# A hybrid recurrent layer: the framework orders the instructions by its other timing model

## The chip, the cores and the metric

The kernel runs on one core of one Trainium2 chip. The metric is the device time of one execution in microseconds (us). Three executions of the kernel before took 660.12, 658.99 and 655.33 us; the median is 658.99.

The core has five engines that run side by side, each from an instruction queue of its own that is worked off strictly in order: TensorE (PE: matmuls; PEld: the loading of a matmul's stationary operand), VectorE (DVE), ScalarE (ACT), GpSimd (POOL) and SyncE (SP), which here only starts transfers (DMA). An instruction that needs another engine's result waits for a semaphore, and all that stands behind it in the same queue waits with it.

## The reference

One layer mixes 1,024 prompt tokens and eight samples of eight tokens each (1,088 tokens of width 1,024). A projection with `w_in` gives the inputs of four mixers and their gates. Mixer A is a causal convolution and a gated linear recurrence (RG-LRU). B is a convolution and a state space model in chunks (SSD). C is a convolution and a gated delta rule in chunks, with one triangular matrix to invert for each chunk and head. D is a complex linear recurrence (S5) with a GELU and a gate. The four gated outputs are put side by side, projected with `w_out`, added to the scaled input and normalised:

```python
z = jnp.einsum('bld,de->ble', x, p['w_in'])
...
ya, conv_a, h_a = rglru_mixer(a_x, conv_a, h_a, p)
yb, conv_b, h_b = ssd_mixer(b_xbc, b_dt, conv_b, h_b, p)
yc, conv_c, s_c = gdn_mixer(c_qkv, c_beta, c_decay, conv_c, s_c, p)
yd, s5_re, s5_im = s5_mixer(d_u, s5_re, s5_im, p)
...
mix = jnp.concatenate([ya, yb, yc, yd], axis=-1).astype(x.dtype)
out = jnp.einsum('ble,ed->bld', mix, p['w_out'])
x = layer_norm(ALPHA * x + out, p['ln_g'], p['ln_b'])
```

Besides the layer's output the new convolution caches and recurrent states are returned. All of it is float32.

## The kernel before

**The large products.** Every float32 operand of a large product is split into two parts, high and low (`xh`, `xl`, `wh`, `wl`), and a product takes three matmuls: lines 261 to 263 for the projection in (tiles `pg`, columns in blocks of 320, 384 and 384, eight k-tiles), lines 438 to 440 for the token-major columns, lines 1511 to 1513 for the projection out. The weights come by DMA into `wr` (two buffers) and are split by ACT (line 157) and DVE (line 158). Two banks of PSUM take the results (`pg`), and ACT or DVE copies them out (lines 277, 279, 1417, 1418).

**The stages.** First come the loads of x, its transposes (line 216) and D's u; then D itself (`s5`), in turn with the token-major columns and the first channel tiles of C; then the decays (`decays`, `softplus`: small DVE steps in a row, lines 337 to 351), and the rest of C's input with its convolutions (lines 299 and 301). From then on two streams are written in turn by `merge`: `gdn` (C's chunks) and `side` (A, then B, the gates, and at the end `project`, the projection out with residual and LayerNorm).

**The chain of C.** For each of nine chunks `invert` doubles an inverse in up to six levels. One level is a chain across engines: PE line 920 (`T`), DVE line 922, two DVE copies line 911 (`tb`), PE lines 925 and 927 (`XY`), ACT line 929, PE line 932, ACT line 933, two DVE copies line 911 (`yb`). Then PE lines 939 to 951 (`E`, `F`) and 961, 964. `state` carries the state from chunk to chunk; `finish` normalises a chunk's output `o`: its factor `ors` is a power taken on POOL (line 1064), DVE applies it (lines 1065, 1068), and PE transposes the result (line 1071, `oT`). `ssd` does the same with `yrs` on POOL (line 1195), DVE line 1196 and the transpose `yT` (line 1200). The LayerNorm of `project` takes its power on POOL too (line 1522), and POOL multiplies and adds two rows of 1,024 (lines 1528 and 1529). A's recurrence needs POOL's line 1295, then a DVE scan (line 1296), then POOL's copies into `hfin` (lines 1297, 1298), which PE transposes (line 1303, `hf`). POOL also copies the convolutions' tails (lines 305, 306), which PE transposes (line 326, `pt`).

**What sets the order.** No order is written out for an engine. The kernel is traced once, and an instruction's place in what was traced is its priority: earlier is more urgent. When the context on line 1569 closes, the framework's planner plays the program on a timing model of the core. Whenever an engine is free in that model, it takes the most urgent of its instructions whose inputs and buffers the model says are ready; an instruction that is less urgent but ready goes ahead of one that still waits. The order in which the model dispatches them is then fixed as the order of each engine's queue on the chip, DMA starts included, and buffers of the rotating pools (for instance the 11 strips of pool `dp`, the two `wr`, the two banks `pg`) are given out in that same order. Data dependencies hold in any order, by semaphores. In the program before, 2,776 of TensorE's 3,806 instructions and 1,380 of DVE's 1,399 stand at another place in their queue than the written order would give them, by 23 and 30 places on average.

The framework has two such models. The default one, used before, is the simpler. The other is called by the framework "the more detailed of its two timing simulators". Of their differences it says that the default one leaves out the fixed cost of GpSimd's elementwise instructions, and that the other takes every table of ScalarE's functions as loaded, so that it sees no cost in a change of tables; the default one does price that.

Of the kernel before, what the change touches and what calls it, by code (L numbers as in the profile page):

```python
# [22 lines left out]
T = NP + NS  # L23
# [10 lines left out]
def seqs(ap):  # L34
    """[p, 88] -> [p, seq, 11]: three cached columns, then eight tokens."""
    return ap.rearrange("p (b e) -> p b e", e=11)
# [7 lines left out]
def hybrid_step(ctx, tc, I, O, dbg=None):  # L44
    nc = tc.nc
# [6 lines left out]
    I = {k: v[0] if k not in ("x_prompt", "x_sample") else v for k, v in I.items()}  # L52
# [51 lines left out]
    def merge(*streams):  # L104
        """Emits several streams in step, each by its share of its own length: (generator, length)."""
        live = [[g, 0.0, w] for g, w in streams]
        while live:
            e = min(live, key=lambda e: e[1] / e[2])
            try:
                c = next(e[0])  # L110
                e[1] += c
                yield c
            except StopIteration:
                live.remove(e)
# [10 lines left out]

# [1 line left out]
    xs2 = I["x_sample"].rearrange("b j d -> (b j) d")  # L127
# [7 lines left out]
    w_in = I["w_in"].rearrange("(k p) e -> p k e", p=P)  # L135
# [3 lines left out]
    def load_w(parts, kn=4, pool=None):  # L139
        """Columns of w_in in two exact parts: the views of each k-tile."""  # L140
        n = sum(b - a for a, b in parts)
# [20 lines left out]

# [1 line left out]
    eps6 = 1e-6  # L164
# [7 lines left out]

# [1 line left out]
    prm = strip(cc, name="prm")  # L174
# [28 lines left out]

# [1 line left out]
    xh = xp.tile([P, 8, T], F32R, name="xh", tag="xh")  # L205
# [13 lines left out]

# [1 line left out]
    pcol = const([P, off[6]], F32, "pcol")  # L221
# [15 lines left out]
    def col(key, i):  # L237
        """Column i of a parameter: channel tile (and tap, for the convs)."""
        j, t = divmod(i, tiles_of.get(key, 6))
        c = off[t] + rows[key] + j  # L240
        return pcol[:, c:c + 1]
# [4 lines left out]

# [1 line left out]
    deep = [0, 0]  # L248
# [32 lines left out]
    def gemm_strip(c0, key, i, pool):  # L281
        """A projected channel tile laid out for the causal conv."""
        s = strip(pool, name="z")
        G.memset(s[:, 0:3], 0.0)
        G.tensor_copy(seqs(s[:, 1027:SW])[:, :, 0:3], cached(key, i))

        def evac(a, b, o):
            if a == 0:
                copy_out(seqs(s[:, 1027:SW])[:, :, 3:11], toks(o[:, :NS]))
                copy_out(s[:, 3:3 + b - NS], o[:, NS:])  # L290
            else:
                copy_out(s[:, 3 + a - NS:3 + b - NS], o)

        yield from gemm_ch(c0 + P * i, evac)
        return s
# [12 lines left out]
    def silu_compact(s, acc):  # L308
        """acc holds half the conv: silu = (tanh(acc) + 1) acc, samples first."""
        a0, s0 = seqs(acc[:, NP:CL])[:, :, 3:11], toks(s[:, 0:NS])  # L310
        act(s0, a0, AF.Tanh)
        act(s[:, NS:T], acc[:, :NP], AF.Tanh)
        stt(s0, s0, 1.0, a0, OP.add, OP.mult)
        stt(s[:, NS:T], s[:, NS:T], 1.0, acc[:, :NP], OP.add, OP.mult)
# [4 lines left out]
    def store_tails(gt, nt, oi):  # L319
        """[p, nt, 27] -> conv caches: three rows of the prompt, 24 of the samples."""  # L320
        t = 0
# [11 lines left out]
    def softplus(x, n):  # L333
        """max(x, 0) + log1p(exp(-|x|)), the log as 2 atanh(u / (2 + u))."""
        nx = small([P, n], name="nx")
# [18 lines left out]
    def exp_fine(o, x, n):  # L354
        """exp to float32's own accuracy: 2^k times a series in the remainder."""
        magic = 1.5 * 2.0 ** 23
# [18 lines left out]
    def rsqrt_fine(o, x, n):  # L375
        """1 / sqrt(x) for positive x: a guess from the exponent, then Newton's steps."""
        b = small([P, n], name="b")
# [10 lines left out]

# [1 line left out]
    ud_d = [dr.tile([P, 8, 136], F32, name=f"dud{i}", tag=f"dud{i}") for i in range(2)]  # L390
# [14 lines left out]
    def u_tiles():  # L405
        """u, its tokens in the order (place in the chunk of 8, chunk), through DRAM to [(s, j), g, c]."""
        us = [strip(dp, name="us")[:, :T].rearrange("p (s c) -> p s c", s=8) for _ in range(2)]
# [18 lines left out]

# [1 line left out]
    raw = const([P, 9, 12], F32, "raw")  # L428
# [21 lines left out]
    def decays(x, bias, na):  # L450
        """softplus(x + bias), its running sum times -a within a chunk, and that sum's exponentials."""
        xb = small([P, 9, 4], name="xb")
# [29 lines left out]

    # ================= D: S5 =================
    magic = 1.5 * 2.0 ** 23
# [3 lines left out]
    def s5(dp):  # L488
# [6 lines left out]
        def cmul(o, a, b, sh, e0=V, e1=V, conj=False):  # L495
            """o = a * b or conj(a) * b, each a pair (re, im)."""
            n = math.prod(sh)
# [57 lines left out]
        act(un[:, 1], rr, AF.Sin)  # L555
        # powers of A = mag * unit: A^0 .. A^8
        pw = early([P, 2, 9, 8], F32, "pw")
# [7 lines left out]

        # f = (A - 1) / lambda and B-bar = f * b
        am = small([P, 8], name="am")
# [21 lines left out]
        for r_ in range(2):  # L589
            for s in range(8):  # L590
                G.tensor_copy(pwr[:, r_, :, s], pw[:, r_, 7 - s])
            V.tensor_copy(pwa[:, r_].rearrange("p q s -> p s q"), pw[:, r_, 1:9])
        # the unit's eighth power, brought back to modulus one
        u2 = small([P, 2, 8], name="u2")
# [10 lines left out]
        for j in range(2):  # L605
            tt(u8[:, j], u8[:, j], nr, OP.mult)
        # C transposed: [(g2, n), ri, q, i], with the imaginary part negated too
        ck = dk("ck")
# [5 lines left out]
        ts(ctr[:, 2], pc[:, P:256], -1.0, None, op0=OP.mult)  # L614
        # D on the diagonal of the zero lag: rows (7, j)
        drow = s5in[:, 514:770]
# [5 lines left out]
        dv = dm.rearrange("p (q g i) -> p q g i", q=8, g=2)  # L622
        # initial states of the samples
        hin = early([P, 2, 64], F32, "hin")
# [12 lines left out]
        def sums(hf):  # L637
            """The stationary operands of the sums into a chunk's end state, and the lags' kernels."""
            q0 = 4 * hf
# [41 lines left out]
        def table(hf):  # L681
            """The unit's powers 8, 16, .. 1024, by doubling."""
            q0 = 4 * hf
# [10 lines left out]
        def half_run(hf, U, lg, lo, tz, tab):  # L694
# [18 lines left out]
            cmul((H[:, 0, :, 9:], H[:, 1, :, 9:]), tab, (gd[:, 0], gd[:, 1]), [4, P], V, V)  # L713
            # states after the last token
            for r_ in range(2):
# [47 lines left out]
        yield  # L763
        # GLU: twice the gated output
        glu = strip(dp, name="glu")[:, :512].rearrange("p (k f) -> p k f", k=2)
# [23 lines left out]

# [1 line left out]
    def gammas(wk, ti, ac, nac, heads, ptag, stag, bufs):  # L791
        """exp(ac_t - ac_s) for t >= s in the same run, else 0: [s, head, t]."""
        n = NS if ti == 0 else P
# [13 lines left out]

    # ================= C: gated DeltaNet =================
    HO = (0, 2, 1, 3)   # order of the heads in a tile of four: by half of the partitions

    def norms(tiles, pool):
        """1 / norm of each head's vector, token-major: [t, chunk, head]."""
        ps = bank("ssq")
# [13 lines left out]
    def gdn(wk, up, q, k, v, rk, rq):  # L827
# [65 lines left out]
        def invert(d):  # L893
            """((I + N)^-1)^T from (I + N)^T: blocks of 64 by doubling in half precision and one correction
            from the exact residual, then the two halves joined."""
            n, A = d["n"], d["A"]
# [207 lines left out]

    # ================= B: SSD =================
    def ssd(wk, up, x, BT, CT):
# [152 lines left out]

    # ================= A: RG-LRU =================  # L1260
    def rglru(wk, up, xc, out):
# [46 lines left out]

# [1 line left out]
    U_ = []  # L1310
# [5 lines left out]

# [1 line left out]
    tri = early([P, P], F32, "tri")  # L1318
# [93 lines left out]
    def gate(c0, pool):  # L1412
        """Twice the silu of a gate's tile."""
        g = strip(pool, name="gate")

        def evac(a, b, o):
            act(g[:, a:b], o, AF.Tanh, scale=0.5)
            stt(g[:, a:b], g[:, a:b], 1.0, o, OP.add, OP.mult)

        yield from gemm_ch(c0, evac)  # L1420
        return g
# [43 lines left out]

# [1 line left out]
    def project():  # L1467
# [105 lines left out]
```

## Time and profile before

| | |
|---|---|
| three executions | 660.12, 658.99, 655.33 us |
| median | 658.99 us |
| profiled execution: span, first to last instruction (the page gives no other time for it) | 655.5 us |
| mean granted TensorE clock, share of full | 0.977 |
| busy: PE, PEld, DVE, ACT, POOL | 610.6, 521.9, 483.0, 274.0, 183.9 us |
| instructions | 12,071 |
| HBM read, written | 32.31, 10.41 MB |

"Busy" is the union of the time in which an engine has an instruction under way; TensorE's matmuls overlap in their pipeline, so a busy TensorE need not be at its peak. A wait of an engine is put down to the instruction that released it. Waits of an engine that is not the bound of a stretch cost nothing by themselves.

### The profile page before, as it was taken

Reading aid. Unit: us, or ns where it says so; the run is one execution under the profiler, and the core shown is the slowest. Engines: PE = TensorE matmul, PEld = TensorE weight load, DVE = VectorE, ACT = ScalarE, POOL = GpSimd, SP = SyncE. Lnnn points to the kernel's source line nnn. Section 1 sums busy time; section 2 is a strip of 40 time slices with the busy share of each in tenths; the row PEclk is TensorE's granted clock in tenths of the full one; section 3 lists DMA queues with packets and bytes.
Section 4 is the critical chain, followed back from the end, with each engine's and each line's share of the span. In section 5 each row is a group of like instructions: output and inputs, shape, how many; then the busy total and the mean of one; then the engine's idle time right before and its main releaser. Section 6 shows DMA issues by size and latency. Waiting matters only on the chain.

```text
span 655.5 us, 12071 instructions
## 1 busy us (share of the span) xinstructions
PE 610.6 (93%) x4394; PEld 521.9 (80%) x4394; DVE 483.0 (74%) x1399; ACT 274.0 (42%) x693; POOL 183.9 (28%) x320
## 2 busy tenths in 40 slices
PE   5999899899999999988999999999999796999995
PEld 5999899899998876777888877778878554678884
DVE  5587999955568677798887687868777887854343
ACT  4343335254434254855444434454443742332210
POOL 7511439300202021232302123023030212443533
PEclk9999989899889999998999999999999997999998
DMA  8655003042411111101111132001022511013122
GB/s 248 164 143 159 17 26 101 0 116 60 111 43 37 34 35 33 33 3 31 34 33 33 37 99 72 17 18 42 9 73 73 170 45 48 13 58 123 70 108 84
DMA packets 52569, 43.49 MB, mean 66 GB/s; under 512 B 17051, under 2 KB 45746, under 8 KB 52510
## 3 DMA queue, kind: packets, MB, share of 16 engines
q1 hardware_dynamic: 51966, 42.53, 22.2%
q8 instruction: 34, 0.56, 0.3%
q0 software_dynamic: 544, 0.19, 0.2%
q14 instruction: 25, 0.20, 0.1%
HBM read 32.31 MB, written 10.41 MB: 65 GB/s over the span
## 4 chain that ended last, share of the span: by engine, by line
PE 69%; DVE 20%; issue 4%; ACT 3%; POOL 2%; DMA 2%; SPq 0%; DVEq 0%; ACTq 0%; POOLq 0%
PE pg L261 10%; PE pg L262 10%; PE pg L263 10%; PE pg L1513 5%; PE pg L1511 5%; PE pg L1512 5%; DVE acc L301 2%; DVE tb L911 2%; DVE yb L911 2%; PE ssq L820 1%; PE px L216 1%; DMA x<-in_x_prompt_dram 1%; PE kq L882 1%; PE yd L1158 1%; PE cb L1147 1%
## 5 line engine op out<-in xcount | busy, mean ns | idle before, releaser
L261 PE MATMUL pg<-xh,wh 128*128 128x384 f32 (+1 forms) x480 | 166.9, 348 | 2.2 <-DVE z L279 2.2
L262 PE MATMUL pg<-xl,wh 128*128 128x384 f32 (+1 forms) x480 | 165.8, 345 | 0.0
L263 PE MATMUL pg<-xh,wl 128*128 128x384 f32 (+1 forms) x480 | 164.5, 343 | 0.0
L261 PEld LDWEIGHTS pg<-xh,wh 128*128 128x128 f32 x480 | 92.8, 193 | 5.1 <-DVE z L279 2.8
L262 PEld LDWEIGHTS pg<-xl,wh 128*128 128x128 f32 x480 | 92.7, 193 | 2.7 <-issue 1.3
L263 PEld LDWEIGHTS pg<-xh,wl 128*128 128x128 f32 x480 | 92.6, 193 | 1.2 <-issue 0.3
L1511 PE MATMUL pg<-woh,wh 128*128 128x512 f32 (+1 forms) x144 | 59.0, 409 | 2.5 <-ACT wh L1500 2.5
L1513 PE MATMUL pg<-woh,wl 128*128 128x512 f32 (+1 forms) x144 | 58.8, 408 | 0.4 <-DVE wl L1501 0.4
L1512 PE MATMUL pg<-wol,wh 128*128 128x512 f32 (+1 forms) x144 | 58.9, 409 | 0.0
L301 DVE SCALAR_TENSOR_TENSOR acc<-z,pcol,acc 128x1112 f32<-128x1112 f32 x36 | 49.7, 1380 | 2.7 <-ACT acc L299 2.5
L157 ACT ACTIVATE wh<-wr 128x512 fp32r<-128x512 f32 (+1 forms) x44 | 27.7, 631 | 48.7 <-PE pg L262 33.2
L158 DVE TENSOR_TENSOR wl<-wr,wh 128x512 fp32r<-128x512 f32 (+1 forms) x44 | 31.5, 717 | 13.4 <-ACT wh L157 12.8
L929 ACT ACTIVATE XY<-XY 128x256 f16<-128x256 f32 (+1 forms) x51 | 19.4, 380 | 51.5 <-PE XY L927 46.1
L1514 DVE SCALAR_TENSOR_TENSOR y<-y,pg 128x512 f32<-128x512 f32 (+1 forms) x18 | 12.3, 686 | 32.7 <-PE pg L1513 29.7
L1511 PEld LDWEIGHTS pg<-woh,wh 128*128 128x128 f32 (+1 forms) x144 | 26.9, 187 | 9.7 <-ACT wh L1500 2.8
L1513 PEld LDWEIGHTS pg<-woh,wl 128*128 128x128 f32 (+1 forms) x144 | 26.8, 186 | 7.6 <-DVE wl L1501 0.9
L1512 PEld LDWEIGHTS pg<-wol,wh 128*128 128x128 f32 (+1 forms) x144 | 26.8, 186 | 6.5 <-issue 0.6
L922 DVE TENSOR_TENSOR T<-T,lev 128x256 f16<-128x256 f32 (+1 forms) x51 | 21.4, 420 | 11.3 <-PE T L920 10.6
L277 ACT ACTIVATE z<-pg 128x384 f32<-128x384 f32 (+2 forms) x37 | 14.2, 393 | 35.3 <-PE pg L263 33.9
L933 ACT ACTIVATE XY<-XY 128x256 f16<-128x256 f32 (+1 forms) x51 | 19.5, 381 | 20.5 <-PE XY L932 20.3
L911 DVE COPY tb<-T 64x256 f16<-64x256 f16 x99 | 26.8, 271 | 1.6
L911 DVE COPY yb<-XY 64x256 f16<-64x256 f16 x99 | 23.8, 240 | 5.2 <-ACT XY L933 3.8
(486 smaller groups left out, 1369.6 us busy)
## 6 DMA issues: line engine op xcount, KB each, us to landing
wr<-in_w_in_dram SPq DMA_DIRECT2D x40, 256.0 KB
x<-in_x_prompt_dram SPq DMA_DIRECT2D x8, 512.0 KB
wo<-in_w_out_dram SPq DMA_DIRECT2D x16, 256.0 KB
y<-in_x_prompt_dram SPq DMA_DIRECT2D x8, 512.0 KB
out_dram<-y SPq DMA_DIRECT2D x7, 512.0 KB
bgd<-bg SPq DMA_DIRECT2D x9, 128.0 KB
dud<-us SPq DMA_DIRECT2D x2, 544.0 KB
U<-dud SPq DMA_DIRECT2D x16, 68.0 KB
```

The source lines that it names most:

```text
L157: act(hv_, wv, AF.Copy)
L158: lo_eng[0].tensor_tensor(lv, wv, hv_.bitcast(F32), OP.subtract)
L261: mm(o, whi[k], xh[:, k, a:b], start=(k == 0), stop=False)
L262: mm(o, whi[k], xl[:, k, a:b], start=False, stop=False)
L263: mm(o, wlo[k], xh[:, k, a:b], start=False, stop=(k == 7))
L301: stt(acc[:, :CL], s[:, j:j + CL], col(wkey, j * nt + i), acc[:, :CL], OP.mult, OP.add)
L911: V.tensor_copy(dst[s, :, s], src[s])
L922: tt(t_[:n], pt[:n], lev[:n, l].unsqueeze(1).to_broadcast([n, 4, 64]), OP.mult)
L933: act(XY[:n, 256:], px[:n, 256:], AF.Copy)
L1511: mm(ps[:n], mh[k_], woh[:, k_, e], start=(k_ == 0), stop=False)
L1512: mm(ps[:n], mh[k_], wol[:, k_, e], start=False, stop=False)
L1513: mm(ps[:n], ml[k_], woh[:, k_, e], start=False, stop=(k_ == 7))
```

## The change

The context that closes over the whole kernel is asked to plan on the other timing model. Comments and docstrings are taken out as well (their lines stay empty, so line numbers agree); no other line of code differs.

```diff
@@ -32,7 +32,7 @@
 def seqs(ap):
-    """[p, 88] -> [p, seq, 11]: three cached columns, then eight tokens."""
+
     return ap.rearrange("p (b e) -> p b e", e=11)
...
@@ -1566,7 +1566,7 @@
         outs.append(nc.dram_tensor(f"out_{i}_dram", shape, F32, kind="ExternalOutput").ap())
-    with tile.TileContext(nc) as tc:
+    with tile.TileContext(nc, schedule_with_timeline_sim=True) as tc:
         hybrid_step(tc, ins, outs)
```

So the same instructions with the same operands are issued: none is added and none is removed by the source. What can differ is the order of each of the five queues, which buffer of a pool a tile gets, the semaphores that follow from the two, and how often ScalarE has to load a function table.

## Rows read from the trace of the kernel before

**Rows 1.** the page, busy time of each engine: us, share of the span, instructions.

```profile
PE 610.6 (93%) x4394; PEld 521.9 (80%) x4394; DVE 483.0 (74%) x1399; ACT 274.0 (42%) x693; POOL 183.9 (28%) x320
```

**Rows 2.** stretches: from:to, length, busy us of each engine (instructions), clock, DMA share, GB/s.

```profile
0.00:20.00 20.00, 13.44 (x69) 12.51 (x70) 12.05 (x36) 9.65 (x18) 14.77 (x38) 1.00 0.72 212
...
75.00:125.00 50.00, 44.61 (x305) 42.47 (x304) 48.85 (x128) 15.35 (x40) 32.93 (x64) 0.93 0.16 47
...
275.00:300.00 25.00, 19.56 (x153) 16.92 (x153) 22.53 (x45) 13.36 (x24) 9.06 (x17) 1.00 0.05 11
...
500.00:550.00 50.00, 40.41 (x280) 28.32 (x281) 42.39 (x126) 25.10 (x74) 11.40 (x10) 0.93 0.27 86
...
640.00:655.50 15.50, 7.86 (x34) 6.00 (x32) 5.77 (x10) 0.67 (x1) 5.79 (x3) 0.89 0.18 69
```

**Rows 3.** the page, chain of work that ended last, shares by engine.

```profile
PE 69%; DVE 20%; issue 4%; ACT 3%; POOL 2%; DMA 2%; SPq 0%; DVEq 0%; ACTq 0%; POOLq 0%
```

**Rows 4.** waits of PE: line, releaser, us in total, times, longest us.

```profile
PE XY L927 <- DVE yb L911: 6.0, 4, 5.0
...
PE XY L932 <- DVE tb L911: 2.5, 3, 1.7
...
PE hf L1303 <- POOL hfin L1298: 2.3, 1, 2.3
...
PE F L947 <- DVE tb L942: 1.8, 4, 0.9
...
PE oT L1071 <- DVE o L1068: 1.6, 2, 1.1
...
PE XY L927 <- DVE T L922: 1.6, 2, 1.2
...
PE pt L326 <- POOL tails L305: 1.3, 2, 0.9
...
PE yT L1200 <- DVE y L1196: 0.6, 2, 0.4
```

**Rows 5.** groups of POOL: line, op, shapes, count, busy us, mean ns, idle before.

```profile
L1529 POOL TENSOR_TENSOR y<-y,ln 128x1024 f32<-128x1024 f32 (+1 forms) x8 | 19.4, 2421 | 0.6
...
L1064 POOL TENSOR_TENSOR ors<-oss,mexp 128x4 f32<-128x4 f32 (+1 forms) x9 | 11.2, 1239 | 28.6 <-DVE oss L1062 28.4
```

**Rows 6.** timeline of POOL from 290 us: start us, us, instruction, idle before.

```profile
294.60 2.05 POOL L1064 TENSOR_TENSOR ors<-oss,mexp 128x4 f32<-128x4 f32 x1 [7.40 <-DVE oss L1062]
296.57 0.23 POOL L1295 COPY gi<-pcol 128x8 f32<-128x8 f32 x1
```

**Rows 7.** timeline of PE, three places.

```profile
299.74 0.28 PE L1303 MATMUL hf<-idf,hfin 128*9 128x128 f32 x1 [2.32 <-POOL hfin L1298]
...
547.58 0.40 PE L927 MATMUL XY<-T,yb 128*128 128x64 f16 x4 [5.03 <-DVE yb L911]
547.79 0.78 PE L1513 MATMUL pg<-woh,wl 128*128 128x512 f32 x1
...
580.49 0.41 PE L1071 MATMUL oT<-idf,o 128*128 128x128 f32 x2 [1.12 <-DVE o L1068]
```

**Rows 8.** timeline of DVE from 542 us.

```profile
542.36 2.51 DVE L911 COPY tb<-T 64x256 f16<-64x256 f16 x2
544.90 2.63 DVE L911 COPY yb<-XY 64x256 f16<-64x256 f16 x2
```

**Rows 9.** timeline of POOL from 542 us.

```profile
542.45 2.33 POOL L1528 TENSOR_TENSOR y<-y,ln 64x1024 f32<-64x1024 f32 x1 [1.54 <-ACT y L1527]
544.86 2.33 POOL L1529 TENSOR_TENSOR y<-y,ln 64x1024 f32<-64x1024 f32 x1
```

**Rows 10.** the page, the copies of line 911 on DVE.

```profile
L911 DVE COPY tb<-T 64x256 f16<-64x256 f16 x99 | 26.8, 271 | 1.6
```

**Rows 11.** groups of ACT, two of nine table loads.

```profile
L554 ACT ACT_TABLE_LOAD x1 | 1.3, 1283 | 0.0
L444 ACT ACT_TABLE_LOAD x1 | 1.3, 1283 | 0.0
```

## The prediction, made before the change was run

> **What bounds the kernel now.** I read the busy times first, then the stretches, then the chain of waits, and last the waits of TensorE one by one. TensorE is busy for 610.6 of 655.5 us [rows 1], so it is without any work for 44.9 us. No change of order can return more than that, except for what hides inside busy time (below). Take the idle time apart by stretch, length minus busy [rows 2]: 6.6 us stand in the first 20 us and 7.6 us in the last 15.5 us, where the loads of x and the last tile's LayerNorm leave nothing to put in; 5.4 us stand between 75 and 125 us, where DVE is busy 48.85 of 50 us and is the bound. That leaves 44.9 - 6.6 - 7.6 - 5.4 = 25.3 us, of which 5.4 us between 275 and 300 us and 9.6 us between 500 and 550 us. The chain that ended last agrees: 69% of it is TensorE and 20% DVE [rows 3].
>
> The waits of TensorE say what those 25.3 us are. They are not waits of the large products for weights, in the main, but small matmuls of a chain that stood at the head of the queue before their input was there [rows 4]: the doubling of C's inverse behind DVE's copies (6.0, 2.5, 1.8 and 1.6 us), and transposes that come after a GpSimd step (`hf` 2.3, `oT` 1.6, `pt` 1.3, `yT` 0.6 us). In the order as it runs, matmuls of the projections stand behind them in the same queue: after the longest of these waits, of line 927 until 547.58 us, the third matmul of an open group follows (line 1513), whose first two ran before the wait [rows 7]. So these are errors of the plan: the model thought the input would be there.
>
> One is easy to follow. At 294.60 us GpSimd starts the power `ors`, which takes 2.05 us although it writes 4 elements a partition; the copy for A's recurrence comes only after it [rows 6], DVE's scan waits for the copy, and the transpose `hf` waits 2.32 us at the head of TensorE's queue [rows 7]. The power takes 1.24 us on average [rows 5]. By the framework's own words the default model leaves out the fixed cost of such GpSimd instructions, the other does not.
>
> **The change, part by part.** No instruction comes or goes by the source. The sum goes against the span of 655.5 us; the median of the executions is 3.5 us above it, and I add those 3.5 us unchanged.
>
> *The written priorities* stay, and with them the coarse course: D, then C's inputs, then the two streams. Cost 0; what covers it is that each stage needs the one before by its data.
>
> *Small matmuls behind GpSimd.* With GpSimd's steps priced, `hf`, `oT`, `pt` and `yT` are dispatched later, and large matmuls go before them. Those waits sum to 2.3 + 1.6 + 1.3 + 0.6 = 5.8 us [rows 4]. I take all of it: -5.8 us. The bounds are 0, if the model prices them no better, and -5.8.
>
> *Small matmuls behind DVE.* The doubling's waits, without the one of 5.0 us, sum to (6.0 - 5.0) + 2.5 + 1.8 + 1.6 = 6.9 us. A model that is closer in DVE's and TensorE's times avoids some and makes others, since a DVE instruction of a long kind can't be interrupted in either plan. I take half: -3.4 us, between -6.9 and +6.9, by the symmetry of exchanging one imperfect plan for another.
>
> *The one wait of 5.0 us* comes from a coincidence of DVE and GpSimd (below, the rival for slower). I take 0: this one is broken up by any new order, and another may arise. Bounds -5.0 and +15, three such for one.
>
> *Large matmuls that wait* for a split weight or a free bank are the rest of the 25.3 us: 25.3 - 5.8 - 6.9 - 5.0 = 7.6 us. Two weight buffers and two banks stay two. 0, at best -7.6.
>
> *SyncE and the transfers.* The starts of the DMAs are reordered too; behind a start that waits for its buffer all later ones wait. The DMA engines are busy 16% to 27% in the stretches that count [rows 2], so bandwidth is no bound; a weight block that comes late would show as a wait of TensorE of the 7.6 us kind. 0.
>
> *Function tables.* Each load takes 1.283 us of ScalarE, and the first needs of a sine and of a tanh are two of nine [rows 11]. The new model sees no cost in a change. ScalarE is busy 274 of 655.5 us, which covers a load, unless it falls into a chain. 0, at worst +5, four more in the chain.
>
> *The clock.* The granted clock is 0.93 in the two stretches with most idle time inside, 1.00 elsewhere [rows 2]. 7% of 50 us at half clock costs 1.75 us of full-speed work; fewer stalls would give it back. 0, at best -3.5 for both.
>
> Sum: 655.5 + 3.5 - 5.8 - 3.4 = 649.8, so **650 us**, 1.4% below the median. The best that the terms allow is 659.0 - 25.3 - 3.5 = 630; nothing in the rows suggests that a planner reaches it.
>
> **The rivals.** *Slower: GpSimd holds up DVE's copies.* Between 542.36 and 547.53 us four copies of line 911 take 2.51 and 2.63 us a pair [rows 8], against 0.27 us for one on average [rows 10]; each pair ends when GpSimd's addition or multiplication over 1,024 columns ends, 2.33 us each [rows 9]. They are links of the doubling, and TensorE stands still for the 5.0 us of [rows 4]. So a coincidence costs about 2.5 us of TensorE. Nothing that the framework says of its models tells that either prices it, so the new order deals these coincidences anew, and there are sixteen such long GpSimd steps (eight of each line; line 1529 takes 19.4 us in all [rows 5]) beside the small ones. Two of the sixteen hit now. With five more hits and none of the gain it is 659.0 + 5 x 2.5 = 671.5 us. It decides from three more hits on (7.5 us, just over 1%), if the gain stays away, and from seven on if the gain comes. Against it: C's last transpose runs at 580.49 us [rows 7], so only the steps of the first tiles, from 542 us on, can meet the chain.
>
> The Trainium skill, "SBUF — State Buffer", section "Who interferes with whom", says that DVE's copies in a two-port mode and GpSimd share a pair of ports as an exclusive lock: whoever issues first has it for the whole instruction, and the other blocks fully. The trace agrees: the pairs of copies end with GpSimd's instruction. By that rule the loss of a hit is the rest of the GpSimd instruction, whichever planner made the order, which speaks against a gain from a better model.
>
> *No change.* The order moves, but each wait that goes makes room for another, because TensorE has 610.6 us of work and the priorities are the same: 659 us, from 652.4 to 665.6. For it: the default order already puts large matmuls between most steps of the chain, as the 25.3 us in 655.5 show. To this belongs that the option changes nothing, the order being decided by priorities and buffers; as the order before differs from the written one in most places and hangs on modelled readiness, I give that 2 in 100.
>
> **How the numbers follow.** About 1% is what a measurement of this kernel can tell from no change. Faster by more (650 us; its own range 634 to 652.4): 0.41. Within 1%: 0.27. Slower by more (671.5; 665.6 to 692): 0.32. Faster is ahead because the waits that the default model explains are in the rows by name, slower close behind because a whole order, with its buffers, is exchanged for one that has never run. The range of 634 to 682 leaves out about 0.07 below and 0.11 above. Cases of both signs hold most of the chance, so the likeliest one's own range stands above.
>
> **What would show it.** In the profile after, the same counts on each engine but ScalarE's table loads. Right: the waits of `hf`, `oT`, `pt`, `yT` behind GpSimd fall from 5.8 to under 2 us, TensorE's idle time between 20 and 640 us, without 75 to 125, from 25.3 to about 16 us, and the busy sum stays near 610. Slower by the coincidences: line 911's mean above 0.27 us, and waits of line 927 or 932 of over 2 us each beside lines 1528 and 1529. Wrong altogether: a fall or rise of TensorE's busy sum itself by more than 10 us, which would say that what matters is inside busy time (how often large and small matmuls alternate), or a wait for weights or for a buffer that isn't there now.

## The result: 17% slower, and what the profile after shows

The changed kernel takes 769.97 us (median of 4 executions, 765.98 to 771.48), the kernel before 658.56 us beside it. The ratio is 1.169, with a 95% interval of 1.163 to 1.175. The prediction said 650 us, at most 682. The profiled execution took 771.48 us, with a span of 769.8 us.

The page of the kernel after: first busy time of each engine (us, share of the span, instructions), which answers to [rows 1]; then, of the view in 40 equal slices, TensorE's busy tenths and its granted clock in tenths; then the shares of the chain that ended last, which answer to [rows 3].

```profile
PE 663.7 (86%) x4394; PEld 575.6 (75%) x4394; DVE 490.2 (64%) x1399; ACT 272.4 (35%) x693; POOL 189.4 (25%) x320
...
PE   6998989769999999999999989879975776857754
...
PEclk9999998969799999999999985869977585675856
...
PE 15%; DVE 10%; issue 9%; ACT 2%; POOL 1%; DVEq 0%; ACTq 0%; POOLq 0%
```

The instructions are as many as before on every engine. The span grew by 769.8 - 655.5 = 114.3 us: TensorE's busy sum rose by 663.7 - 610.6 = 53.1 us and its idle time from 44.9 to 106.1 us. Both stand in the right third of the slices, where the clock digits fall to 5 to 8. The chain of waits could be followed over 37% of the span only, so it is no guide here.

The stretches of the kernel after (from:to, length, busy us of each engine with its instructions, clock, DMA share, GB/s), answering to [rows 2]:

```profile
275.00:300.00 25.00, 25.00 (x152) 20.80 (x149) 21.73 (x30) 15.73 (x24) 13.95 (x15) 1.00 0.11 28
300.00:500.00 200.00, 192.18 (x1356) 161.69 (x1355) 147.79 (x425) 87.35 (x256) 40.75 (x62) 0.93 0.19 54
500.00:550.00 50.00, 45.61 (x256) 35.37 (x255) 28.44 (x84) 14.50 (x40) 17.21 (x11) 0.86 0.27 86
550.00:640.00 90.00, 65.44 (x415) 52.28 (x414) 51.22 (x150) 21.86 (x67) 23.27 (x20) 0.73 0.12 41
640.00:769.80 129.80, 84.77 (x494) 68.00 (x491) 65.36 (x187) 25.52 (x81) 20.58 (x20) 0.63 0.05 17
```

The stretch of the kernel before that [rows 2] do not show:

```profile
300.00:500.00 200.00, 194.61 (x1603) 162.29 (x1600) 159.11 (x484) 90.88 (x271) 40.99 (x66) 0.99 0.15 43
```

From 275 to 550 us TensorE is about as busy as before: 25.00, 192.18 and 45.61 us, against 19.56, 194.61 and 40.41. A reader who stops there would call it the better plan. But it is full of the wrong work. The next rows are the times of one line on TensorE (count, min/median/max ns, first and last start): the in-projection's second product, which from C's start on belongs to the stream beside C, and C's last transpose. The kernel after:

```profile
L262 PE MATMUL pg<-xl,wh x480: 302/337/667, 13.6 to 423.1; 128*128 128x384 f32 x101, 128*128 128x320 f32 x59
L1071 PE MATMUL oT<-idf,o x18: 216/421/475, 369.3 to 753.2; 128*128 128x128 f32 x16, 64*128 64x64 f32 x2
```

The kernel before:

```profile
L262 PE MATMUL pg<-xl,wh x480: 303/337/669, 17.0 to 512.1; 128*128 128x384 f32 x101, 128*128 128x320 f32 x59
L1071 PE MATMUL oT<-idf,o x18: 216/273/329, 274.1 to 580.6; 128*128 128x128 f32 x16, 64*128 64x64 f32 x2
```

There the in-projection ends 68 us ahead of C, in the kernel after 330 us ahead: the large products are spent 89 us earlier, and C's first chunk is done 95 us later, its last 173 us later. From some 550 us on C's last chunks have nothing beside them but the projection out of the tile just finished.

How C fell behind is seen on TensorE's timeline of the kernel after from 327 us (start us, us, instruction):

```profile
327.83 0.28 PE L920 MATMUL T<-XY,ah 128*128 128x64 f16 x4
327.95 0.42 PE L262 MATMUL pg<-xl,wh 128*128 128x384 f32 x1
...
332.43 0.34 PE L263 MATMUL pg<-xh,wl 128*128 128x384 f32 x1
...
332.71 0.28 PE L927 MATMUL XY<-T,yb 128*128 128x64 f16 x4
...
337.08 0.29 PE L932 MATMUL XY<-XY,tb 128*128 128x64 f16 x4
337.21 0.28 PE L920 MATMUL T<-XY,ah 128*128 128x64 f16 x4
...
342.48 0.29 PE L927 MATMUL XY<-T,yb 128*128 128x64 f16 x4
```

And on DVE's timeline of the same kernel, the copies into `yb`, the last input that each of the two steps of line 927 needs (the other, `T`, was written just before; the copies into `tb` are for line 932):

```profile
328.88 0.44 DVE L911 COPY yb<-XY 64x256 f16<-64x256 f16 x2
...
338.33 0.45 DVE L911 COPY yb<-XY 64x256 f16<-64x256 f16 x2
```

Between 327.95 and 332.43 us stand 26 large products, then 24, then 29. The input of line 927 was there at 329.32 us, yet it ran at 332.71; the second time it was there at 338.78 and ran at 342.48. TensorE was busy all the time from 327 to 343 us, 16.00 of 16 us. **No wait shows any of this:** the step is not waiting for data, it stands behind products that were put into the queue before it. One round from line 920 to the next takes 9.4 us. In the kernel before, at the same time of the run, it takes 2.1 us, with 3 to 5 large products between links:

```profile
327.60 0.28 PE L920 MATMUL T<-XY,ah 128*128 128x64 f16 x4
...
328.78 0.29 PE L927 MATMUL XY<-T,yb 128*128 128x64 f16 x4
...
329.54 0.28 PE L932 MATMUL XY<-XY,tb 128*128 128x64 f16 x4
329.65 0.28 PE L920 MATMUL T<-XY,ah 128*128 128x64 f16 x4
...
331.77 0.28 PE L920 MATMUL T<-XY,ah 128*128 128x64 f16 x4
```

What TensorE waited for, over the whole span of the kernel after (us in total, times, longest), answers to [rows 4]:

```profile
PE XY L927 <- DVE yb L911: 20.0, 14, 2.9
PE o L1046 <- DVE S L1042: 9.3, 5, 2.2
PE XY L932 <- ACT XY L929: 9.3, 17, 0.8
PE pg L261 <- ACT z L277: 6.6, 1, 6.6
...
PE oT L1071 <- DVE o L1068: 5.5, 2, 3.7
```

`hf` and `pt` behind GpSimd are gone from the longest ones, as forecast (though not for the reason given, see below), and it does not matter: C's own links took their place, in the time when little else is left to run (18.8 of the 20.0 us for `yb` lie after 550 us).

### The profile page after: what moved, and what is told of

It is laid out like the page before. It is cut to its first block, busy times and chain, and to the rows that moved or that the text cites. A ratio compares the mean times of both kernels' runs of the same rounds, so it can differ in the third digit from the quotient of the medians.

```text
span 769.8 us, 12105 instructions
## 1 busy us (share of the span) xinstructions
PE 663.7 (86%) x4394; PEld 575.6 (75%) x4394; DVE 490.2 (64%) x1399; ACT 272.4 (35%) x693; POOL 189.4 (25%) x320
## 5 line engine op out<-in xcount | busy, mean ns | idle before, releaser
L1511 PE MATMUL pg<-woh,wh 128*128 128x512 f32 (+1 forms) x144 | 64.1, 445 | 1.4 <-ACT wh L1500 1.1
L1512 PE MATMUL pg<-wol,wh 128*128 128x512 f32 (+1 forms) x144 | 62.5, 434 | 0.1
L158 DVE TENSOR_TENSOR wl<-wr,wh 128x512 fp32r<-128x512 f32 (+1 forms) x44 | 33.4, 758 | 42.2 <-ACT wh L157 39.5
L911 DVE COPY yb<-XY 64x256 f16<-64x256 f16 x99 | 40.5, 409 | 1.4
L1511 PEld LDWEIGHTS pg<-woh,wh 128*128 128x128 f32 (+1 forms) x144 | 30.0, 209 | 9.4 <-ACT wh L1500 1.7
L1513 PEld LDWEIGHTS pg<-woh,wl 128*128 128x128 f32 (+1 forms) x144 | 28.8, 200 | 9.0 <-DVE wl L1501 1.7
L1512 PEld LDWEIGHTS pg<-wol,wh 128*128 128x128 f32 (+1 forms) x144 | 29.6, 205 | 7.5 <-DVE wol L1478 0.6
L927 PE MATMUL XY<-T,yb 128*128 128x64 f16 (+1 forms) x168 | 14.5, 218 | 20.0 <-DVE yb L911 20.0
L927 PEld LDWEIGHTS <-yb 128*128 128x128 f16 (+1 forms) x168 | 10.4, 114 | 27.6 <-DVE yb L911 23.4
```

The lines of the kernel that those rows point to most:

```text
L158: lo_eng[0].tensor_tensor(lv, wv, hv_.bitcast(F32), OP.subtract)
L911: V.tensor_copy(dst[s, :, s], src[s])
L927: mm(pX[:n, h], idh[:n, :n] if Y is None else yb[:n, h, :n], t_[:n, h], start=False, stop=False, skip_group_check=True)
L1511: mm(ps[:n], mh[k_], woh[:, k_, e], start=(k_ == 0), stop=False)
L1512: mm(ps[:n], mh[k_], wol[:, k_, e], start=False, stop=False)
L1513: mm(ps[:n], ml[k_], woh[:, k_, e], start=False, stop=(k_ == 7))
```

## The experiments

**Theory W (window).** The other model has, besides its prices, an issue window for each engine: the number of instructions that its sequencer may have committed, in order, ahead of execution. The framework sets it to 35 on TensorE and 12 elsewhere. While an input of C's chain is not there in the model, the planner fills TensorE's window with ready products; when the input comes, the most urgent instruction stands behind up to 35 others. A planner that chooses when the engine is free has no such delay. **Rivals:** the model's prices in general (P), of GpSimd alone (G), C's rank in the written order (M), and the late start of C.

The edit of the first three runs is two lines ahead of the context, with N = 8, 2 and 1:

```diff
+    from concourse.hw_specs import TRN2Spec as _spec
+    _spec.ENG_ISSUE_QUEUE_DEPTH = {**_spec.ENG_ISSUE_QUEUE_DEPTH, mybir.EngineType.PE: N}
```

> Same timing model as the changed kernel; only the number of TensorE instructions that the model lets its sequencer commit, in order, ahead of execution is cut from 35 to 8. Theory W (window): what costs the time is that a step of C becomes ready after up to 35 TensorE instructions have been placed ahead of it, however low their priority. With 8 it stands behind some 8 instead of 27 to 29 large matmuls, so the in-projection's last matmul moves from 422.6 back towards 511.6 us, C's last oT from 752.6 towards 580, and the time falls by over half of the loss: 690 us, 665 to 715. Theory P (the model's prices of the operations, not the window): the time stays at 770 us, within 2 per cent.

Measured: 665.9 us (664.9 to 667.4), ratio to before 1.011 [1.006, 1.016]. The in-projection's line 262 ends at 480.1 us, C's `oT` at 647.0. W's direction, and more of it than forecast: 104 of 111 us are back.

> As before with a window of 2. Theory W: 662 us, 650 to 680, TensorE's busy sum back from 663.7 to 605 to 625 us, its clock back over 0.95. Theory P: 770 us, within 2 per cent.

Measured: 666.8 us (661.8 to 668.0), 1.011 [1.006, 1.017]; TensorE busy 607.4 us, clock 0.971. As W said; P as the cause of the whole loss is out, since every price is unchanged.

> As before with a window of 1: each TensorE instruction is picked when the one ahead is done. Theory W: as the kernel before, 645 to 667 us, though the model's prices are still the other ones; this is also the only fair test of what the prediction forecast (650 us) for the prices alone. Theory P: 770 us, within 2 per cent.

Measured: 870.0 us (868.6 to 870.6), 1.321 [1.316, 1.326]. Both theories missed. By my count of the plan, which no trace can confirm, it is nearly the written order: 1,410 of TensorE's 3,806 instructions stand elsewhere than written, by 4 places on average, against 2,776 by 23 before. On the chip the steps come too close, and TensorE waits for them; its longest waits in this run:

```profile
PE XY L927 <- DVE yb L911: 23.7, 23, 5.0
PE pg L261 <- DVE z L279: 14.6, 2, 13.0
PE XY L927 <- DVE T L922: 13.4, 10, 3.3
```

In all it is idle for 868.7 - 704.9 = 163.8 us. My guess is that with one place the model lets no TensorE instruction overlap the next, so that TensorE looks slow and all else early; that was not tried. So the smallest window is not the best one. This run was to show what the other model's prices do alone, and it does not show it.

The fourth run leaves the windows and takes GpSimd's prices away:

```diff
+    _spec.GPSIMD_OP_FIXED_NS_AND_CYCLES_PER_ELEMENT = {k: (0, 0.1) for k in _spec.GPSIMD_OP_FIXED_NS_AND_CYCLES_PER_ELEMENT}
```

> The changed kernel with its window of 35, but the model prices every GpSimd operation at nearly nothing (no fixed time, 0.1 cycles an element). Theory W: 770 us, within 1.5 per cent, oT's last start within 10 us of 752.6. Theory G (steps fed by GpSimd are priced long in the other model, so that C's chain is planned late): under 720 us, with C's chunks closer than 47.6 us.

Measured: 770.2 us (one execution). `oT` starts last at 751.5 us, and C's late chunks stay 47.5 us apart. G is out: the one difference of the models that I built on moves nothing measurable at a window of 35. With a short window the prices were not varied.

A window of 16 on TensorE gives another point of the curve.

> Window of 16 in place of 35 on TensorE, all else as in the changed kernel. In the plan the median count of large matmuls between neighbouring links of C's chain is 12 (20 with 35, 8 with 8, 7 with 2, 4 in the kernel before). Theory W (window): the time follows that count between the runs at 8 (666 us) and 35 (770 us): 705 us, 680 to 735. Rival T (a threshold: only when the whole in-projection is spent before C's seventh chunk does it cost anything): at or near one of the two ends, under 675 or over 755 us.

Measured: 725.9 us (one execution), inside W's range, well away from both ends of T. Line 262 ends at 449.7 us, `oT` at 706.9.

Next all windows at 2, and TensorE's at 4:

```diff
+    _spec.ENG_ISSUE_QUEUE_DEPTH = dict.fromkeys(_spec.ENG_ISSUE_QUEUE_DEPTH, 2)
```

> A window of 2 on every engine, not on TensorE alone. If the windows of 12 on VectorE, ScalarE and GpSimd had a part in what is left of the loss at TensorE's window of 2 (667 against 659 us), the time comes to 659 us or below and C's first kt starts before 210 us (201 in the kernel before, 215 with TensorE's window at 2). If what is left comes from the model's other prices in the first 200 us, it stays at 667 us, within 1 per cent, and kt's first start at 213 to 217 us.

Measured: 653.0 us (649.8 to 654.3), 0.992 [0.989, 0.995]: 0.8% below the kernel before, clear of noise. The time says that the other windows cost something (667 to 653), but C's first `kt` still starts at 216.9 us: what they cost lies later, and the loss of the first 200 us is another matter.

> TensorE's window at 4, between the two runs that gave 667 (2) and 666 us (8). Theory W with the loss of the first 200 us unchanged: 664 us, 655 to 670. A version that beats the kernel before would need under 652 us; I give that 1 chance in 10.

Measured: 664.5 us, 1.011 [1.006, 1.016]; as expected.

The counts and times by TensorE's window (median number of large products between neighbouring links where any stand, in TensorE's queue; last start of line 262 and of C's `oT`; median time, us):

```text
window of TensorE   between links   L262 last   oT last   time
35 (as changed)          20           423.1      753.2    770.0
16                       12           449.7      706.9    725.9
 8                        8           480.1      647.0    665.9
 4                        7           491.9      626.5    664.5
 2                        7           510.9      607.2    666.8
 2, all engines at 2      5           513.9      582.5    653.0
kernel before             4           512.1      580.6    658.6
```

The time does not follow the count all the way. With TensorE's window at 2, 4 and 8 it stays at 664.5 to 666.8 us, though C's last `oT` moves from 607.2 to 647.0 us, to within 19 us of the end. C's lateness costs nothing until it reaches the end of the program; from there on, with 8, 16 and 35, the time moves with `oT`, 17 to 19 us behind it. So rival T put its threshold in the wrong place, but there is one.

The written order could perhaps be suited to the window. The eighth run raises C's weight in the last line:

```diff
-    run(merge((gdn(wk, up, q, k, v, *rn), 130.0), (side(), 280.0)))
+    run(merge((gdn(wk, up, q, k, v, *rn), 260.0), (side(), 280.0)))
```

> The changed kernel with its window of 35, and C's weight in the last line's merge doubled from 130 to 260, so that C's instructions come earlier in the written order and have the better priority. Theory W: priority can't pass what has been committed; while large matmuls last, C's links stay some 5 us apart and its chunks over 50 us, and once C has used its places the rest has no chain to fill: over 700 us. Rival M (the written weights no longer suit the model's prices, so that C is only ranked too low): C's chunks come 42 us apart or less from the first and the time falls under 680 us.

Measured: 831.8 us (one execution). The gain that M forecast did not come. But the run tests less than it was meant to. C is at first as late as in the changed kernel (`oT` first at 372.5 us, against 369.3); then it runs alone until 616.7 us, and the rest runs after it. SyncE's timeline shows one thing that kept the rest away:

```profile
370.94 0.34 SPq L1459 DMA_DIRECT2D yD<-zdd  x1
609.29 0.38 SPq L1103 DMA_DIRECT2D out_dram<-Sout  x1
```

Line 1103 stores C's last state, which DVE's line 1102 had written at 609.25 us. In this order the store stands in SyncE's queue right behind a transfer that started at 370.94 us, so for 238 us that queue starts no other, and the DMA share below is 0.00. What made this run slow is that store at least in part; whether a higher rank helps without it was not tried, so M stays open as a remedy, and W's figure of over 700 us held partly by luck.

This run shows C by itself; its stretches, columns as above:

```profile
400.00:500.00 100.00, 58.55 (x489) 48.29 (x488) 48.56 (x178) 27.03 (x84) 12.05 (x18) 0.59 0.00 1
500.00:550.00 50.00, 33.99 (x236) 28.59 (x235) 23.47 (x86) 12.09 (x40) 8.02 (x12) 0.50 0.00 1
```

and two of its `oT` steps on TensorE's timeline:

```profile
449.81 0.69 PE L1071 MATMUL oT<-idf,o 128*128 128x128 f32 x2 [0.86 <-ACT qd L1009]
...
517.01 0.67 PE L1071 MATMUL oT<-idf,o 128*128 128x128 f32 x2
```

Two chunks in 67.2 us are 33.6 us for one, with the clock at 0.50 to 0.59, that is mostly at the lower of its two levels (1.2 and 2.4 GHz). In the tail of the changed kernel the same steps stand 47.6 us apart, and the projection out of one tile lies between them:

```profile
662.59 0.69 PE L1071 MATMUL oT<-idf,o 128*128 128x128 f32 x2 [0.85 <-ACT qd L1009]
664.66 0.78 PE L1511 MATMUL pg<-woh,wh 128*128 128x512 f32 x1
...
678.35 0.40 PE L1513 MATMUL pg<-woh,wl 128*128 128x512 f32 x1
...
710.21 0.69 PE L1071 MATMUL oT<-idf,o 128*128 128x128 f32 x2 [0.85 <-ACT qd L1009]
```

678.35 + 0.40 - 664.66 = 14.1 us, and 33.6 + 14.1 = 47.7. So in the tail chain and products run nearly one after the other, at a granted clock of 0.64. The sum is an estimate: one round of the doubling gets through between the products, and one step waits 2.9 us for a long copy behind them. Before, chain and products ran through each other.

There remains the start of C, 14 to 19 us late in every plan of the other model so far (64 with the window of one). DVE's timeline of the run with all windows at 2 shows a place (in brackets: idle before, and what ended it):

```profile
64.76 0.43 DVE L447 SCALAR_TENSOR_TENSOR bg<-bg 128x256 f32<-128x256 f32 x1 [1.71 <-ACT bg L444]
...
69.93 0.43 DVE L447 SCALAR_TENSOR_TENSOR bg<-bg 128x256 f32<-128x256 f32 x1 [3.82 <-ACT bg L444]
...
76.26 1.29 DVE L505 TENSOR_TENSOR ab<-cm,cm 128x512 f32<-128x512 f32 x2
...
80.92 0.23 DVE L686 COPY tab<-u 128x4 f32<-128x4 f32 x2
```

Six steps of line 447 stand in DVE's queue, each waiting for ScalarE's line 444, 13.0 us in all, and behind five of them D's `ab`, behind all six `kk` and `tab`. In the kernel before, `tab` stands 15 us earlier:

```profile
65.96 0.23 DVE L686 COPY tab<-u 128x4 f32<-128x4 f32 x2
```

The next edit gives D's part the higher priority:

```diff
-        lg0 = sums(0)
-        lg1 = sums(1)
-        tab0 = table(0)
+        with tc.high_priority():
+            lg0 = sums(0)
+            lg1 = sums(1)
+            tab0 = table(0)
```

> Window of 2 on every engine, and D's sums and first table (L649 to L655, L686) written with high priority, so that they stand ahead of the six L447 steps which, in every plan of the other model, VectorE runs first while it waits 13.0 us in pieces for ScalarE's L444. If that place is the loss of the first 200 us: the first table starts at 66 to 70 instead of 81 us, C's first kt at 203 to 209 instead of 216.5, and the time falls from 653 to 640 to 648 us. If the loss is elsewhere: kt stays over 213 us and the time at 653 us, within 0.7 per cent.

Measured: 641.2 us (639.2 to 643.7), **0.973 [0.969, 0.977]**. `tab` starts at 64.8 us, `kt` at 204.5. The edit moves D's steps ahead on every engine, not on DVE alone; with that said, the place is shown, and it gives back 11.8 us. This version beats both kernels.

```profile
PE 599.0 (94%) x4394; PEld 518.0 (81%) x4394; DVE 477.5 (75%) x1399; ACT 276.7 (43%) x695; POOL 189.4 (30%) x320
```

> The kernel before (its own timing model) with the same priority for D. There the table already starts at 66.0 us, so if the place is the cause there is nothing to win: 657 us, within 0.7 per cent. If the priority helps for another reason it gains here too, by 1 per cent or more.

Measured: 657.1 us, 0.9965 [0.9937, 0.9993]: under the 1% that would count, as expected where `tab` was early already.

> The changed kernel with its windows of 35 and 12 and the same priority for D. Theory W (the window starves C between 260 and 560 us): kt's first start comes some 10 us earlier than 220 us, but C is still starved while large matmuls last, so the time stays at 755 to 772 us. If the late start of C were what set the whole loss going: under 720 us.

Measured: 752.9 us (one execution), 2 us under W's range. `kt` starts at 201.9 instead of 220.6 us, and the end moves by 17 us, nearly as much. The late start is a separate part of the loss, and the smaller one; line 262 still ends at 404.5 us, and C is still starved.

> TensorE's window left at 35, the windows of all other engines at 2: the fourth corner beside 770 (35 and 12), 667 (2 and 12) and 653 us (2 and 2). Theory W, that TensorE's window makes the loss: 755 to 772 us. If the other windows carried as much of it: under 730 us.

Measured: 761.5 us (one execution); line 262 ends at 426.7 us. So TensorE's window is worth about 108 us with the others at 2 (761.5 - 653.0) and 103 with the others at 12 (770.0 - 666.8); the others' windows are worth some 9 to 14, a rough figure, since the four executions of the changed kernel alone spread over 5.5 us.

**What is settled:** the loss is the look-ahead of TensorE's queue in the planning model, for about 103 of 111 us; D's place behind line 447 is worth some 12 to 17 us in these plans (the parts overlap and are no sum); GpSimd's prices are worth nothing at a window of 35. **What stays open:** what the other model's prices are worth alone, at a short window; why a window of one gives nearly the written order; which of the other three windows gives the last 14 us; and why the model puts line 447 ahead of D. The last was not traced to a price.

## Why the prediction was wrong, step by step

*The bound.* The reading that TensorE's work fills the kernel before holds. But of the 25.3 us of idle time that were to be had, the best run here returned little: at 641.2 us it has TensorE idle for 637.5 - 599.0 = 38.5 us in its span, 6.4 less than before, while the busy sum fell by 610.6 - 599.0 = 11.6 us. Most of its gain lies in busy time, which the bound set aside. And a bound on the gain is none on the loss; I used it for the scale of both.

***The written priorities: the step that failed.*** I took the coarse course as given, at a cost of 0, "what covers it is that each stage needs the one before by its data". That holds within a stream. Between the two streams of the last line no data decide who goes first until the projection out, only priorities, and these count only among instructions that are ready at the moment of choice. I knew that the moment of choice belongs to the model and asked only what the models charge for an instruction, not when they choose. With 35 places chosen ahead, the side stream overtook C. Measured, this step costs about 103 us.

*Small matmuls behind GpSimd, -5.8 us.* `hf` and `pt` did vanish from the waits; `oT` rose from 1.6 to 5.5 us. But the prices are not what removed them: with GpSimd priced at nearly zero they are gone as well, and the time stays at 770.2 us, while with full prices and TensorE's window at 2 they stand again:

```profile
PE pt L326 <- POOL tails L305: 1.7, 1, 1.7
...
PE hf L1303 <- POOL hfin L1298: 1.0, 1, 1.0
```

*Small matmuls behind DVE, -3.4 us.* The bound of +6.9 was drawn from the waits of a kernel in which large products stood between the links. Without them the waits of line 927 for `yb` alone are 20.0 us.

*The coincidence and the rival for slower.* The mechanism is there, as a follower. Ten copies of line 911 take over 0.6 us, four before, and eight of the ten come after 550 us, where the LayerNorm of one tile meets C's next chunk: DVE's and GpSimd's timelines of the kernel after, answering to [rows 8] and [rows 9],

```profile
581.41 4.68 DVE L911 COPY yb<-XY 64x256 f16<-64x256 f16 x2
```

```profile
581.18 2.40 POOL L1528 TENSOR_TENSOR y<-y,ln 128x1024 f32<-128x1024 f32 x1 [1.55 <-ACT y L1527]
583.66 2.34 POOL L1529 TENSOR_TENSOR y<-y,ln 128x1024 f32<-128x1024 f32 x1
```

The pair of copies ends at 586.09 us, with GpSimd's second instruction at 586.00 us. That agrees with the lock which the Trainium skill, "SBUF — State Buffer", section "Who interferes with whom", states for such copies and GpSimd. Over the 0.21 us of an undisturbed copy, the long ones sum to 20.2 us, 6.9 before: 13 us of copies, of 111 us of loss; what they cost in time no run shows. The rival's reason against itself, that only the first tiles can meet the chain, fell with the order. The mean of the copies into `yb` shows it (count, busy us, mean ns); [rows 10] have those into `tb`. The kernel after, then the kernel before:

```profile
L911 DVE COPY yb<-XY 64x256 f16<-64x256 f16 x99 | 40.5, 409 | 1.4
```

```profile
L911 DVE COPY yb<-XY 64x256 f16<-64x256 f16 x99 | 23.8, 240 | 5.2 <-ACT XY L933 3.8
```

The one wait of 5.0 us did not return as one piece; the longest of line 927 is now 2.9 us. So the rival's sign was right, and its price of 671.5 us was that of a small part of what happened.

*The clock, 0 with a gain at best.* The granted clock over the span fell from 0.977 to 0.855, and the busy sum rose by 53.1 us with the same instructions. How much of the 53.1 us is the clock is not shown, since small matmuls that run alone also overlap less: at 327.83 us line 920 takes 0.28 us and the next product starts 0.12 us later (above), while at 684.88 us its 0.40 us stand alone, before 0.90 us of idle time. The clock was low where TensorE's work had thinned out (busy 65.4 of 90 us at 0.73, 84.8 of 129.8 us at 0.63, above); with windows of 8 and below, one excepted, it is back at 0.95 to 0.98. So it came with the starving; that it only followed is argued. My sum was off too: 0.93 over 50 us lacks 0.07 x 50 = 3.5 us in each stretch, 7 for both and not 3.5, and the clock was not 1.00 elsewhere, but 0.89 in the last row of [rows 2].

*Large matmuls that wait, transfers and function tables, 0 each.* Nine loads of tables as before [rows 11], no wait for weights over 1.3 us. One large product does wait longer than before, 6.6 us for a bank that ScalarE frees late; the same wait stands in the runs with 667, 666 and 653 us.

*What would show it* named the right alarm: a busy sum that moves by more than 10 us, "how often large and small matmuls alternate". I wrote that as a sign of error and gave it neither a price nor a chance. It could have been priced from the rows of before: C's chain stands 306 us from first to last `oT` (274.1 to 580.6), and if the side stream gets ahead, whatever of C is left then runs with little beside it.

## What to carry to other kernels

An order is made by when a planner chooses as much as by what it charges: where a latency chain shares an in-order queue with plenty of ready bulk work, what is placed ahead of time stands in front of the chain's next link. Here that cost nothing more from 2 places to 8, and 104 us from 8 to 35. Look for it by counting bulk instructions between neighbouring links, since no list of waits shows it, and compare where both streams end. Then shorten the look-ahead before touching priorities: raising the chain's rank gave 832 us instead of 770, in a run in which one store of the chain's last state held up all transfers for 238 us, while a priority at one place, where a queue stood behind a waiting instruction, gave 12 us.

## What the runs showed of the hardware that was not expected

C's chain takes 33.6 us a chunk alone with TensorE's clock at 0.50 to 0.59, and in the kernel before 39 us on average in the mixture at nearly full clock (`kt` from 201.6 to 514.3 us, eight steps): alone at little over half the clock it is faster than in the mixture. No run shows it alone at full clock. And a busy share does not tell two orders apart: between 300 and 500 us the kernel after was busy for 192.2 us against 194.6 before, but with 1,356 instructions against 1,603 (clock 0.93 against 0.99). Last, one start of a transfer whose data came late kept every later transfer of SyncE's queue waiting for 238 us.
